# Retention and output projection of the first layer, put into the fixed order of a step pipeline

## The chip, the cores and the metric

The kernel runs on one NeuronCore of a Trainium2 chip. TensorE (PE) multiplies matrices into PSUM, VectorE (DVE) and ScalarE (ACT) work on elements, GpSimd (POOL) issues the stores here, SyncE (SP) issues the loads. The metric is the time of one execution in device microseconds. Before the change it is 2261.67 us, the median of three runs (2260.89 to 2261.71).

## The reference

A trunk of two layers over 512 tokens of width 2048, in float32. The first layer is multi-scale retention with 8 heads, the second is latent attention with 16 heads. What the change touches is the middle and the end of the first layer:

```python
def retention_branch(h, pos, w_in, gn_g, w_out):
    proj = h @ w_in                                  # 2048 -> 2048 q, 2048 k, 4096 v, 4096 g
    q, k, v, g = jnp.split(proj, ...)
    q = rope(q.reshape(B, S, RET_HEADS, RET_DK), pos)             # 8 heads of 256
    k = rope(k.reshape(B, S, RET_HEADS, RET_DK), pos) * (RET_DK ** -0.5)
    y = chunkwise_retention(q, k, v)                 # per head: (q k^T * decay) v, values of 512
    y = (y - mu) * lax.rsqrt(var + EPS)              # per head and token
    y = y.reshape(B, S, RET_WIDTH) * gn_g
    return (jax.nn.silu(g) * y) @ w_out              # 4096 -> 2048

    x = x + gate * y                                 # then the second layer's norm
```

The gate, and the shift and scale of each layer's norm, are products of a conditioning vector with `ada_w`, of which each layer has 2048 x 6144.

## The kernel before, in words

**Number format.** Each float32 operand is split into a high part and a low part (`split`, L132: ACT casts the high part, DVE subtracts for the low part). A product is three matmuls: high by high, high by low, low by high (`mm3`, L157).

**Units and steps.** Weights come in units of 512 KB: a load into a raw tile (three buffers), a split into `whi` and `wlo` (three buffers each), and 24 matmuls of 128x512. The projection into q, k, v and g of heads 0 to 7 (q and k of heads 0 to 5 only) is written as a list of `Step` objects (L619), each with a load, a prepare (the split), a multiply and a follow (the emptying of finished sums). A loop (L873) walks the list. In round i it traces, one after the other, the load of unit i + 3, the prepare of unit i + 1, the multiply of unit i, one row of a later modulation, and the follow of unit i.

**What sets an order.** The program is traced first, and a planner then puts the instructions of each engine into an order, by readiness in its own estimate of time and by the order of tracing. `behind(...)` (L414) takes this freedom away: all instructions traced in its block on the named engines are queued behind the last instruction that was traced on the same engine before the block. Instructions within one block stay free against each other. Each engine then works through its queue strictly in order; a wait holds everything behind it.

**The stretch of the change.** After the loop come three parts with no such order, left to the planner:

- q and k of heads 6 and 7 (`queries_and_keys`, L1023), 16 units.
- `retention(h)` (L923), a generator that is advanced at fixed units of the projection beside it (tables at L1035 and L1210). Its parts: load q and k, rotary product (`rope_halves`), gates' load; scores in 4 PSUM banks, times decay, split; values v loaded and split; y in 4 banks, statistics, group norm (`yn`), times gate; 16 transposes into 4 banks, scaled into `y2` (two buffers) and stored to `y2_d` in HBM.
- `out_projection` (L1047), called for n = 0 to 3. Call n multiplies two heads' `y2` (4 input units, loaded back from `y2_d` and split) with 1024 rows of the output weight, in four rounds r of 512 columns (4 units each) with 4 token banks each. Its partial sums go to `x1` in SBUF (ACT copy, L1063) and are put back into a bank when the next n needs them (ACT copy, L1103). Call n = 3 is final: rounds 0 and 1, then rounds 2 and 3 together in 8 wide units; it multiplies with the gate, adds the residual, squares for the norm and stores. Where a bank was last written by something else, a filling matmul (L1102) writes it whole before the copy; there are 8. While call n runs, heads 2n + 2 and 2n + 3 go through retention.

Banks: 4 in `acc` for the projections, 4 in `aux` for retention. The first matmul of a round needs the refilled bank; the refill needs the bank emptied. `x1_token` and `h2_pair` (L1148) finish a block of tokens: normalise, transpose, apply the second layer's scale and shift.

Of the kernel before, what the change touches and what calls it, by code (L numbers as in the profile page):

```python
# [16 lines left out]
P = 128  # L17
# [32 lines left out]
def hybrid_trunk_kernel(  # L50
# [568 lines left out]
    class Step:  # L619


        def __init__(self, load, prepare, multiply, follow=None, rows=0, sums=None, banks_free=False):
            self.load, self.prepare, self.multiply, self.follow = load, prepare, multiply, follow
            self.rows, self.sums, self.banks_free = rows, sums, banks_free

# [237 lines left out]
    later = later_modulation(lpp, [(i, s_, n) for i, s_ in ((0, 2), (1, 0)) for n in range(2)])  # L863
    fetched = []
    for i in range(3):
        with behind(S_):
            steps[i].load()
    queued(steps[0].prepare)
# [4 lines left out]
    for i, step in enumerate(steps):  # L873
        clock[0] = i
        if i + 3 < len(steps):
            with behind(S_):
                steps[i + 3].load()
        if i + 1 < len(steps):
            with behind(V_, A_):
                steps[i + 1].prepare()  # L880
# [16 lines left out]
        with behind(V_, A_):  # L897
            step.follow()
    assert next(later, None) is None and not fetched
    sum_modulation(0)  # L900
    use_modulation()
    lp.__exit__(None, None, None)


    l1 = tc.tile_pool(name="l1", bufs=1)
    l1p = l1.__enter__()

    cos, sin = rot(l1p, "cos"), rot(l1p, "sin")
    for n, t in enumerate((cos, sin)):
        nc.sync.dma_start(t, tables_d[n * P : (n + 1) * P, :])  # L910

    def rope_halves(b1, b2, dst1, dst2, name):
        t1, t2, t3, t4 = (tmp(f"{name}_t{i}") for i in range(4))
        DVE.tensor_mul(t1, b1, cos)
        DVE.tensor_mul(t4, b1, sin)
        DVE.tensor_mul(t2, b2, sin)
        DVE.tensor_mul(t3, b2, cos)
        DVE.tensor_sub(t1, t1, t2)
        split(t1, dst1[:, 0, :], dst1[:, 1, :])
        DVE.tensor_add(t3, t3, t4)  # L920
        split(t3, dst2[:, 0, :], dst2[:, 1, :])

    def retention(h, own, own2=None):  # L923

        def fetch(src_d, r0, tag, bufs, name):
            t = l1p.tile([P, T], F32, tag=tag, bufs=bufs, name=name)
            nc.sync.dma_start(t, src_d[r0 : r0 + P, :])
            return t

        dec = l1p.tile([P, T], F32, tag="dec", bufs=1, name=f"dec_{h}")  # L930
        nc.sync.dma_start(dec, decay[h])
        qk = []
        for n in range(2):
            raws = [fetch(qk_d, (4 * h + 2 * n + j) * P, "ld", 4, f"qk_{h}_{n}_{j}") for j in range(2)]
            dst = [(own2 or own)(f"qk_{h}_{n}_{j}p") for j in range(2)]
            rope_halves(*raws, *dst, f"rope_{h}_{n}")
            qk.append(dst)
        q, k = qk
        sg = [fetch(g_d, h * T + j * P, "sg", 5, f"sg_{h}_{j}") for j in range(4)]
        yield  # L940
        s_hl = []
        for m in range(NT):
            n = T - m * P
            ps = aux(f"s_{h}_{m}")
            for j in range(2):
                mm3(
                    ps[:, :n],
                    act_block(k[j], m),
                    (q[j][:, 0, m * P :], q[j][:, 1, m * P :]),
                    j == 0, j == 1,  # L950
                )
            st = tmp(f"s_{h}_{m}f")
            DVE.tensor_mul(st[:, :n], ps[:, :n], dec[:, :n])
            if m < 3:
                dst = k4b(f"sT_{h}_{m}")
                s_hl.append((dst[:, 0, :n], dst[:, 1, :n]))
                if m == 1:
                    spare = dst
            else:
                s_hl.append((spare[:, 0, 384:512], spare[:, 1, 384:512]))  # L960
            split(st[:, :n], *s_hl[m])
        v = []
        for t in range(NT):
            raw = fetch(v_d, h * T + t * P, "ld", 4, f"v_{h}_{t}r")
            v.append(own(f"v_{h}_{t}"))
            split(raw, v[t][:, 0, :], v[t][:, 1, :])
        yield
        ys, stats = [], small(f"bn_{h}", 2 * NT)
        for i in range(NT):
            ps = aux(f"y_{h}_{i}")  # L970
            for m in range(i + 1):
                o = (i - m) * P
                mm3(ps, (s_hl[m][0][:, o : o + P], s_hl[m][1][:, o : o + P]), act_row(v[m]), m == 0, m == i)
            st = l1p.tile([P, 6], F32, tag="st6", bufs=4, name=f"st_{h}_{i}")
            DVE.bn_stats(out=st, in_=ps)
            DVE.bn_aggr(out=stats[:, 2 * i : 2 * i + 2], in_=st)
            ys.append(ps)
        var = small(f"var_{h}", NT)
        DVE.tensor_copy(var, stats.rearrange("p (i s) -> p i s", s=2)[:, :, 1])
        r = rsqrt(var, NT, 1.0, f"gn_{h}")  # L980
        nmr = small(f"nmr_{h}", NT)
        DVE.scalar_tensor_tensor(
            out=nmr, in0=stats.rearrange("p (i s) -> p i s", s=2)[:, :, 0], scalar=-1.0, in1=r,
            op0=ALU.mult, op1=ALU.mult,
        )
        yn = []
        for i in range(NT):
            y = l1p.tile([P, T], F32, tag="yn", bufs=4, name=f"yn_{h}_{i}")
            ACT.activation(y, ys[i], AF.Identity, bias=nmr[:, i : i + 1], scale=r[:, i : i + 1])
            if h > 0:  # L990
                DVE.tensor_mul(y, y, sg[i])
            yn.append(y)
        yield
        for j in range(4):
            ps = aux(f"yT_{h}_{j}")
            for i in range(NT):
                PE.transpose(ps[:, i * P : (i + 1) * P], yn[i][:, j * P : (j + 1) * P], ident)
            y2 = l1p.tile([P, T], F32, tag="y2", bufs=2, name=f"y2_{h}_{j}")
            gn = gn_c[:, h * 4 + j : h * 4 + j + 1]
            if h > 0:  # L1000
                ACT.activation(y2, ps, AF.Identity, scale=gn)
            else:
                DVE.scalar_tensor_tensor(out=y2, in0=ps, scalar=gn, in1=sg[j], op0=ALU.mult, op1=ALU.mult)
            r0 = (h * 4 + j) * P
            POOL.dma_start(y2_d[r0 : r0 + P, :], y2)
        yield

    def hooks(table, otherwise=None):
        def each(i):
            if otherwise is not None and i not in table:  # L1010
                otherwise()
            for gen in table.get(i, ()):
                next(gen, None)

        return each

    n_odd = [0]

    def odd(name):
        n_odd[0] += 1  # L1020
        return l1p.tile([P, 2, T], F32R, tag="odd1" if n_odd[0] > 2 else "odd0", bufs=2, name=name)

    def queries_and_keys(h, each, evac):  # L1023
        run(
            chunk(
                [(lambda u=u: load_w(qk_parts(h, u), 2, 512, f"qk{h}_{u}"), [2 * u, 2 * u + 1]) for u in range(8)],
                [acc(f"qk{h}_{b}") for b in range(4)],
                lambda w, ki, kt, b: w_block(w, ki, b), lambda w, ki, kt, b: act_row(hT[kt]), evac,
            ),
            each=each,  # L1030
        )

    r_ = (retention(0, k4), retention(1, k4, odd))
    for h, table in (
        (6, {0: r_[:1], 3: r_, 5: r_[:1], 7: r_}),  # L1035
        (7, {1: r_[1:], 3: r_[1:]}),
    ):

        def qk_keep(b, ps, h=h):
            st = tmp(f"qk{h}_st{b}") if h == 6 else l1p.tile([P, T], F32, tag="yn", bufs=4, name=f"qk{h}_st{b}")  # L1040
            ACT.copy(st, ps)
            POOL.dma_start(qk_d[(4 * h + b) * P : (4 * h + b + 1) * P, :], st)

        queries_and_keys(h, hooks(table), qk_keep)
# [131 lines left out]
    def x1_token(t):  # L1176
# [5 lines left out]
        if t == 2:  # L1182
            h2_pair(0, 0, 8)
# [349 lines left out]
```

## Time and profile before

| | |
|---|---|
| median of three runs | 2261.67 us |
| profiled execution | 2259.02 us, span 2257.2 us |
| TensorE busy | 2190.1 us, 97% of the span |
| VectorE, ScalarE busy | 1514.2 us (67%), 1006.8 us (45%) |
| granted clock of TensorE | 0.995 of full speed |
| the stretch of the change | 948.3 us (first product of q and k of head 6) to 1510 us (last product of the output projection) |

A row of a group of instructions reads: line, engine, operation, tile written from tiles read, shapes, how many; then busy time in us and mean ns of one; then how long the engine was idle just before them, and which engine, tile and line ended that. A row of the order in time begins with the start and the duration, both in us from the start of the span, and has the idle time before it in square brackets. [...]

### The profile page before, as it was taken

What the parts mean: (1) busy time and instruction counts of PE and PEld (TensorE: products, weight loads), DVE (VectorE), ACT (ScalarE), POOL (GpSimd) and SP (SyncE); (2) the same over time, 40 slices, a digit from 0 to 9 for tenths busy, and PEclk for the clock granted to TensorE, in tenths of its full rate; (3) what the DMA queues carried; (4) which work ended last, traced back from release to release, by engine and by line L of the source; (5) the groups of instructions that cost most, each with busy time, mean ns of one, the idle gap of its engine ahead of it and who ended that gap; (6) DMA issues with size and microseconds to landing.
All of it is one profiled execution on the core that took longest, in us unless ns stands there. A gap on an engine that the chain in (4) does not pass through costs nothing.

```text
span 2257.2 us, 28012 instructions
## 1 busy us (share of the span) xinstructions
PE 2190.1 (97%) x10202; PEld 1817.5 (81%) x10202; DVE 1514.2 (67%) x2242; ACT 1006.8 (45%) x1510; POOL 132.7 (6%) x237
## 2 busy tenths in 40 slices
PE   5999999999999999999999999999999999999997
PEld 4887888888888888878878888778888888888886
DVE  7988867676676789675677673455454377777545
ACT  5664433434343444444445454554322255555433
POOL 1000000100000000001000000010000000000000
PEclk9999999999999999999999999999999999999999
DMA  9974685767767678766767664542466432235433
GB/s 342 348 238 161 197 292 188 267 209 252 237 221 251 222 246 277 259 222 197 250 214 244 209 204 141 180 147 89 134 221 224 155 102 80 85 99 175 153 120 117
DMA packets 243564, 449.73 MB, mean 199 GB/s; under 512 B 22024, under 2 KB 95840, under 8 KB 243424
## 3 DMA queue, kind: packets, MB, share of 16 engines
q1 hardware_dynamic: 228016, 400.88, 54.6%
q0 software_dynamic: 14976, 46.78, 5.3%
q8 instruction: 80, 1.31, 0.2%
q14 instruction: 60, 0.49, 0.1%
q10 hardware_dynamic: 432, 0.27, 0.0%
HBM read 396.98 MB, written 50.87 MB: 198 GB/s over the span
## 4 chain that ended last, share of the span: by engine, by line
PE 64%; issue 14%; DVE 8%; DMA 8%; ACT 5%; POOL 1%; SPq 0%; ACTq 0%; POOLq 0%; DVEq 0%
PE o L159 4%; PE o L160 4%; PE o L161 4%; PE qk L161 3%; PE qk L160 3%; PE qk L159 3%; PE g L159 3%; PE g L161 3%; PE g L160 3%; DMA aw<-in_ada_w_dram 2%; PE x L692 2%; PE y L693 2%; PE x L693 2%; PE y L691 2%; PE y L692 2%
## 5 line engine op out<-in xcount | busy, mean ns | idle before, releaser
L159 PE MATMUL o<-o_w_hi,o_h 128*128 128x512 f32 x768 | 301.8, 393 | 8.4 <-ACT o L1103 7.2
L160 PE MATMUL o<-o_w_lo,o_h 128*128 128x512 f32 x768 | 299.2, 390 | 0.0
L161 PE MATMUL o<-o_w_hi,o_l 128*128 128x512 f32 x768 | 299.0, 390 | 0.0
L134 DVE TENSOR_TENSOR o_w_lo<-o_w_raw,o_w_hi 128x1024 fp32r<-128x1024 f32 x96 | 117.3, 1223 | 129.3 <-ACT o_w_hi L133 129.2
L159 PEld LDWEIGHTS o<-o_w_hi,o_h 128*128 128x128 f32 x768 | 144.2, 188 | 42.1 <-ACT o L1103 9.8
L161 PEld LDWEIGHTS o<-o_w_hi,o_l 128*128 128x128 f32 x768 | 144.2, 188 | 30.7 <-DVE o_l L134 0.6
L160 PEld LDWEIGHTS o<-o_w_lo,o_h 128*128 128x128 f32 x768 | 144.3, 188 | 28.7
L826 DVE SCALAR_TENSOR_TENSOR mod_am<-mod_aw,cact,mod_am 128x1024 f32<-128x1024 f32 x120 | 153.6, 1280 | 12.4 <-DMA mod_aw<-in_ada_w_dram 11.8
L133 ACT CAST o_w_hi<-o_w_raw 128x1024 fp32r<-128x1024 f32 x96 | 101.1, 1054 | 110.2 <-PE o L161 91.2
L161 PE MATMUL qk<-hT,qk_l 128*128 128x512 f32 x320 | 125.0, 391 | 0.4 <-DVE qk_l L134 0.4
L159 PE MATMUL qk<-hT,qk_h 128*128 128x512 f32 x320 | 125.4, 392 | 0.0
L160 PE MATMUL qk<-hT,qk_h 128*128 128x512 f32 x320 | 124.5, 389 | 0.0
L134 DVE TENSOR_TENSOR o_l<-o_in,o_h 128x1024 fp32r<-128x1024 f32 x40 | 49.0, 1225 | 86.0 <-ACT o_h L133 85.9
L159 PE MATMUL g<-h,g_hi 128*128 128x512 f32 x256 | 100.6, 393 | 1.1 <-ACT ckv_n L1230 1.1
L160 PE MATMUL g<-h,g_hi 128*128 128x512 f32 x256 | 99.6, 389 | 0.0
L161 PE MATMUL g<-h,g_lo 128*128 128x512 f32 x256 | 99.6, 389 | 0.0
L134 DVE TENSOR_TENSOR g_lo<-g_raw,g_hi 128x1024 fp32r<-128x1024 f32 x32 | 39.2, 1225 | 81.0 <-ACT g_hi L133 81.0
L370 DVE SCALAR_TENSOR_TENSOR am<-aw,cact,am 128x512 f32<-128x512 f32 x118 | 88.7, 752 | 3.6
L133 ACT CAST g_hi<-g_raw 128x1024 fp32r<-128x1024 f32 x32 | 33.7, 1053 | 114.2 <-PE g L160 106.2
L133 ACT CAST o_h<-o_in 128x1024 fp32r<-128x1024 f32 x40 | 42.0, 1052 | 90.1 <-PE o L160 61.2
L133 ACT CAST qk_h<-qk_r 128x1024 fp32r<-128x1024 f32 x40 | 41.4, 1050 | 83.8 <-PE qk L160 70.5
L134 DVE TENSOR_TENSOR qk_l<-qk_r,qk_h 128x1024 fp32r<-128x1024 f32 x40 | 48.7, 1222 | 37.4 <-ACT qk_h L133 37.4
(1355 smaller groups left out, 5678.6 us busy)
## 6 DMA issues: line engine op xcount, KB each, us to landing
mod_aw<-in_ada_w_dram SPq DMA_DIRECT2D x128, 512.0 KB, 5.1
aw<-in_ada_w_dram SPq DMA_DIRECT2D x128, 256.0 KB, 6.0
o_w_raw<-in_ret_w_out_dram SPq DMA_DIRECT2D x64, 512.0 KB, 4.4
qk_r<-in_ret_w_in_dram SPq DMA_DIRECT2D x80, 256.0 KB, 4.0
g_raw<-in_mla_w_in_dram SPq DMA_DIRECT2D x32, 512.0 KB, 3.7
o_w_raw<-in_mla_w_out_dram SPq DMA_DIRECT2D x32, 512.0 KB, 3.7
qk_raw<-in_ret_w_in_dram SPq DMA_DIRECT2D x48, 256.0 KB, 3.9
qk_d<-qk_st POOLq DMA_DIRECT2D x32, 256.0 KB, 4.1
```

The lines of the kernel that those rows point to most:

```text
L133: ACT.copy(hi, src)
L134: DVE.tensor_sub(lo, src, hi.bitcast(F32))
L159: PE.matmul(o, lhs[0], rhs[0], start=first and not seeded, stop=False, skip_group_check=seeded)
L160: PE.matmul(o, lhs[0], rhs[1], start=False, stop=False, skip_group_check=seeded)
L161: return PE.matmul(o, lhs[1], rhs[0], start=False, stop=last, skip_group_check=seeded)
L370: DVE.scalar_tensor_tensor(out=am, in0=aw[:, k % 2], scalar=ck, in1=am, op0=ALU.mult, op1=ALU.add)
L691: PE.matmul(banks[b], a[0], w[0], start=first, stop=False, skip_group_check=True)
L692: PE.matmul(banks[b], a[0], w[1], start=False, stop=False, skip_group_check=True)
L693: PE.matmul(banks[b], a[1], w[0], start=False, stop=True, skip_group_check=True)
L826: DVE.scalar_tensor_tensor(out=am, in0=aw, scalar=ck, in1=am, op0=ALU.mult, op1=ALU.add)
```

## The change

The three parts become steps of the same loop.

- q and k of heads 6 and 7 are 16 more steps. The output projection is 4 blocks of 16 steps, one unit each (`round_steps`; in the last block, 4 steps for the wide units and 4 that finish one block of tokens each, `one_token`).
- A step may carry work beside its own, in three lists: `load` (SP), `form` (DVE and ACT) and `multiply` (TensorE).
- `retention(h)` returns ten pieces. `place` puts them into ten steps of a block that follow one another: the first head of a block from step 0, the second from step 6.
- The rows of the remaining modulation are fetched for fixed steps (`light`).
- The output projection's input units go to a tile of their own with one buffer (`in`), before three raw buffers that they shared with the weights. They are loaded two steps ahead of their use.
- Emptying and refill of a bank are in the follow of a round's last step. In the last block, 4 of the 8 filling matmuls are left out, residuals and gates are loaded at fixed steps, and the first half of the first transposes stands ahead of the last 12 products.

```diff
+        return [
+            {"load": lambda: load_qk(0)},
+            {"load": lambda: load_qk(1), "form": lambda: rope(0, 0)},
+            {"form": lambda: rope(0, 1)},
+            {"load": lambda: load_v(0), "form": lambda: rope(1, 0)},
+            {"load": load_gates, "form": lambda: rope(1, 1), "multiply": scores},
+            {"load": lambda: load_v(2), "form": decay_scores},
+            {"form": split_v, "multiply": values},
+            {"form": group_norm},
+            {"form": gate, "multiply": transposes},
+            {"form": store},
+        ]
...
+    def kept_then(n, r, after):
+        def done(t):
+            keep_sums(n, r, t)
+            if after[0] > 0:
+                seed(*after, t)
+
+        return done
+
+    for n in range(3):
+        block = []
+        for r in range(4):
+            block += round_steps(n, r, kept_then(n, r, (n, r + 1) if r < 3 else (n + 1, 0)))
+        for i in range(2):
+            place(retention(2 * n + 2 + i, big), block, 6 * i)
+        light(block, (0, 1, 2, 3, 4, 6, 9, 10, 12, 14, 15))
+        steps += block
...
+    def o1_input(n, u):
+
+        raw = []
+        r0 = (4 * n + u) * 2 * P
+
+        def load():
+            raw.append(l1_tile("in", 1, f"o1_in{n}_{u}", (P, 2, T)))
+            nc.sync.dma_start(raw[0], y2_d[r0 : r0 + 2 * P, :].rearrange("(k p) n -> p k n", p=P))
+
+        def prepare():
+            o1_in[n, u] = big(f"o1_h{n}_{u}"), big(f"o1_l{n}_{u}")
+            split(raw[0], *o1_in[n, u])
+
+        return load, prepare
...
+            load, prepare = o1_input(n, u)
+            i = n_o1 + 16 * n + u
+            steps[i - 2].beside["load"].append(load)
+            steps[i].units[0] = (steps[i].units[0][0], lambda a=steps[i].units[0][1], b=prepare: (a(), b()))
...
+    def one_token(t, r):
+        if (t, r) == (3, 3):
+            queued(h2_pair, 0, 0, 8)
+        for u in range(4, 8):
+            o1_product(3, wide[u][0], u, 0, t, r, slice((r - 2) * T, (r - 1) * T), u == 7)
...
     for i, step in enumerate(steps):
         clock[0] = i
...
+        with behind(S_):
+            while n_loaded < min(n_prepared + 3, len(loads)):
+                loads[n_loaded]()
+                n_loaded += 1
+            for load in step.beside["load"]:
+                load()
+        n_prepared += prepare_for(i + 1)
+        with behind(V_, A_):
+            use_modulation()
+            for form_ in step.beside["form"]:
+                form_()
+        with behind(T_):
+            if step.banks_free:
+                sum_modulation()
+        with behind(T_):
+            step.multiply()
+        with behind(T_):
+            for multiply in step.beside["multiply"]:
+                multiply()
         with behind(V_, A_):
             for add in fetched:
                 add()
...
+        with behind(V_, A_, T_):
             step.follow()
```

More of the change, by code (lines that the diff above doesn't have):

```diff
@@ L861, in use_modulation, with l1_tile, odd @@
             POOL.dma_start(gate_d[i : i + 1, part : part + 512], row[0:1, :])
-    later = later_modulation(lpp, [(i, s_, n) for i, s_ in ((0, 2), (1, 0)) for n in range(2)])
-    fetched = []
[L865 to L868, printed above, removed]
+    pools = {}
+    def l1_tile(tag, bufs, name, shape=(P, T), dt=F32):
+        return pools["l1"].tile(list(shape), dt, tag=tag, bufs=bufs, name=name)
+    def odd(name):
+        n_odd[0] += 1
+        return l1_tile("odd1" if n_odd[0] > 2 else "odd0", 2, name, (P, 2, T), F32R)
@@ new lines, in place, with light @@
+    def place(pieces, block, first):
+        for i, piece in enumerate(pieces):
+            for kind, fn in piece.items():
+                block[first + i].beside[kind].append(fn)
+    def light(block, which):
+        for i in which:
+            block[i].rows = 1
+        for i in range(4):
+            block[i].banks_free = True
+    block = []
+    for h in (6, 7):
+        block += plain_steps(
+            8, 2, qk_parts_of(h), 512, f"qk{h}", acc, 4,
+            lambda w, ki, kt, b: w_block(w, ki, b), lambda w, ki, kt, b: act_row(hT[kt]),
+            lambda b, ps, h=h: keep_rows(
+                ps, qk_d, (4 * h + b) * P, f"qk{h}_st{b}",
+                own=tmp if h == 6 else lambda name: l1_tile("yn", 4, name),
+            ),
+        )
@@ new lines, in hybrid_trunk_kernel, with x1_block, seed @@
+    n_p = len(steps)
+    light(block, ())
+    place(retention(0, k4), block, 0)
+    place(retention(1, k4, odd), block, 6)
+    steps += block
+    x1 = []
+    ss1 = [small(f"x1_ss{t}", 4) for t in range(NT)]
+    NU1 = 4
+    def x1_block(t, r):
+        if not x1:
+            x1.extend([k4(f"x1_{t_}_{j}", F32) for j in range(2)] for t_ in range(NT))
+        return x1[t][r // 2][:, r % 2, :]
+    o1_banks = {}
+    def seed(n, r, t):
+        o1_banks[n, r, t] = (aux if n == 3 and r % 2 else acc)(f"o1_{n}_{r}_{t}")
+        if n > 0:
+            ACT.copy(o1_banks[n, r, t], x1_block(t, r))
@@ new lines, in o1_product, with round_steps, multiply, follow @@
+    def o1_product(n, w, kt, ki, t, r, cols=slice(0, T), last=False):
+        hi, lo = o1_in[n, kt // 2]
+        a = tuple(p[:, kt % 2, t * P : (t + 1) * P] for p in (hi, lo))
+        o = o1_banks[n, r, t]
+        first = n == 0 and kt == 0
+        for i, j in ((0, 0), (0, 1), (1, 0)):
+            PE.matmul(
+                o, a[i], w[j][:, ki, cols], start=first and i + j == 0, stop=last and i == 1, skip_group_check=True
+            )
+    def round_steps(n, r, done):
+        res = []
+        for u in range(NU1):
+            w, unit = o1_unit(n, r, u, 2, T)
+            step = Step()
+            step.units = [unit]
+            def multiply(u=u, w=w):
+                order = [(ki, t) for ki in range(2) for t in range(NT)]
+                if u in (0, NU1 - 1):
+                    order = [(ki, t) for t in range(NT) for ki in range(2)]
+                for ki, t in order:
+                    if (n, r, t) not in o1_banks:
+                        seed(n, r, t)
+                    o1_product(n, w, 2 * u + ki, ki, t, r, last=u == NU1 - 1 and ki == 1)
+            def follow(u=u):
+                if u == NU1 - 1:
+                    for t in range(NT):
+                        done(t)
+            step.multiply, step.follow = multiply, follow
+            res.append(step)
+        return res
@@ new lines, in kept_then @@
+    def kept_then(n, r, after):
[5 more added lines that the diff above has]
+    for n in range(3):
+        block = []
+        for r in range(4):
[3 more added lines that the diff above has]
+        light(block, (0, 1, 2, 3, 4, 6, 9, 10, 12, 14, 15))
+        steps += block
@@ L912, in rope_halves @@
[L912 to L1044, printed above, removed]
+    assert next(later, None) is None and not fetched and not ripe and not summed
```

306 lines of the change are left out of this document (231 added, 75 removed).

## The prediction

> **What bounds the kernel now.** I read the page's head and its engine line first, then the busy time in two stretches (the input projection of layer 1, which already runs as a step pipeline, and the stretch that the change rewrites), then what TensorE's instructions waited for there, then the order in time of single engines, and the chain that ended last.
>
> ```profile
> span 2257.2 us, 28012 instructions
> PE 2190.1 (97%) x10202; PEld 1817.5 (81%) x10202; DVE 1514.2 (67%) x2242; ACT 1006.8 (45%) x1510; POOL 132.7 (6%) x237
> ```
> ```profile
> 250.00:850.00 600.00, 600.00 (x2641) 495.49 (x2640) 432.52 (x487) 245.34 (x291) 34.35 (x64) 1.00 0.71 236
> 948.30:1510.00 561.70, 548.29 (x2539) 454.55 (x2539) 346.92 (x521) 256.84 (x395) 41.15 (x66) 1.00 0.62 206
> ```
> (Columns: the stretch, its length, then busy time of PE, weight loads, DVE, ACT and POOL, the granted clock, the share of DMA.) TensorE is the bound. The old step pipeline never lets it idle; the rewritten stretch is idle for 561.7 - 548.3 = 13.4 us. The groups that waited (last column: idle before them):
> ```profile
> L159 PE MATMUL o<-o_w_hi,o_h 128*128 128x512 f32 x512 | 201.7, 394 | 8.4 <-ACT o L1103 7.2 <-ACT x L1063 1.0 <-ACT qk_st L1041 0.2
> L1156 PE MATMUL x1T<-ident,x 128*128 128x128 f32 x64 | 11.1, 297 | 4.7 <-DVE h2f L1173 3.3 <-DVE o_g L1071 1.4
> ```
> Most of it is the refill of a sum's bank by ScalarE (L1103). TensorE's busy time overstates its work, because matmuls overlap. The order in time gives the real pace:
> ```profile
> 944.85 3.63 PE L839 MATMUL mod_ps<-ones,mod_am 128*128 128x1 f32 x32
> ...
> 949.59 0.63 PE L160 MATMUL qk<-hT,qk_hi 128*128 128x512 f32 x1
> ...
> 954.17 0.39 PE L159 MATMUL qk<-hT,qk_hi 128*128 128x512 f32 x1
> ...
> 966.18 0.39 PE L161 MATMUL qk<-hT,qk_lo 128*128 128x512 f32 x1
> 966.41 0.39 PE L159 MATMUL s<-qk_0p,qk_0p 128*128 128x512 f32 x1
> ...
> 967.83 0.50 PE L161 MATMUL s<-qk_0p,qk_0p 128*128 128x512 f32 x1 [0.80 <-DVE qk_0p L134]
> ...
> 971.25 0.45 PE L159 MATMUL qk<-hT,qk_hi 128*128 128x512 f32 x1
> ...
> 1001.38 1.91 PE L997 MATMUL yT<-ident,yn 128*128 128x128 f32 x16
> ```
> 54 products start in 954.17 to 966.18: one each 0.2266 us. So a unit of weights (24 products) is 5.44 us of TensorE, the values of a head (30) 6.8, its scores 971.25 - 966.41 - 0.8 - some 0.1 = 3.9, its transposes 1.91 less some 0.2 of overlap, 1.7. Everything below is measured against these 5.44 us, not against 24 x 0.39 = 9.4.
>
> **What it removes.** Work of the stretch, counted from the code: 384 qk, 1536 o, 240 y and 8 filling products (L1102), 2168 x 0.2266 = 491.3; scores 8 x 3.9 = 31.2; transposes 8 x 1.7 = 13.3; some 32 small sums like those at 944.85, 3.6; the first x1 transposes, about 2. Together 541.4, of 561.7: 20.3 us are lost, the 13.4 of idle and 6.9 that busy time hides. About 4 of these I leave standing, an estimate, for the changes from one kind of product to another, which stay. So at most 16.3 us go, and 4 of the 8 filling products, 4 x 0.23 = 0.9: **-17.2 us**.
>
> **What it costs nothing.** Splits, rotary products, gates and loads keep their number and sizes; they run on queues with idle time (DVE 347 and ACT 257 of 562). That cover is gone wherever one queue must finish a list inside one step, which is the next part. The modulation rows move to fixed steps (33 places for 32 rows); their sums stay 128x1 products. The first x1 transposes move in front of the last 12 products of o; they are paid either way, between -4.7 (the idle shown goes) and +3.3 (its h2f part comes again); I take 0. POOL keeps its queue; it only issues.
>
> **What it adds.** In each step DVE and ACT now take, in order: split of the next unit, the retention pieces, the modulation row, and only then the emptying of the sums (follow). What is late in a piece holds the sums, and these hold TensorE. Paces of these engines, by starts in a row:
> ```profile
> 1188.05 0.68 DVE L134 TENSOR_TENSOR v<-v_2r,v 128x512 fp32r<-128x512 f32 x1
> 1188.65 0.68 DVE L134 TENSOR_TENSOR v<-v_3r,v 128x512 fp32r<-128x512 f32 x1
> 1189.33 1.23 DVE L134 TENSOR_TENSOR o_l<-o_in,o_h 128x1024 fp32r<-128x1024 f32 x1
> 1190.47 1.28 DVE L826 SCALAR_TENSOR_TENSOR mod_am<-mod_aw,cact,mod_am 128x1024 f32<-128x1024 f32 x1
> 1191.67 1.22 DVE L134 TENSOR_TENSOR o_w_lo<-o_w_raw,o_w_hi 128x1024 fp32r<-128x1024 f32 x1
> ```
> ```profile
> 1182.17 1.11 ACT L1103 COPY o<-x 128x512 f32<-128x512 f32 x2
> 1183.21 0.59 ACT L1063 COPY x<-o 128x512 f32<-128x512 f32 x1
> ```
> DVE: 0.60 for a 512-wide operation, 1.14 for the low part of a unit, 1.20 for a row. ACT: 0.5 for a copy. The store, an input load's cycle, and the group norm:
> ```profile
> 1349.21 1.26 ACT L1001 ACTIVATE y<-yT,vcol 128x512 f32<-128x512 f32 x2
> ...
> 1355.55 0.69 ACT L1001 ACTIVATE y<-yT,vcol 128x512 f32<-128x512 f32 x1 [3.00 <-DMA y_d<-y]
> ...
> 1356.85 0.69 ACT L1001 ACTIVATE y<-yT,vcol 128x512 f32<-128x512 f32 x1
> ```
> ```profile
> 1047.17 3.70 DMA o_in<-y_d
> 1050.89 1.07 ACT o_h L133
> 1051.98 1.24 DVE o_l L134
> ```
> ```profile
> DMA to landing us min/median/max: 2.3/4.0/7.2
> ```
> ```profile
> 1152.68 0.17 DVE L976 BATCH_NORM_AGGREGATE bn<-st 128x2 f32<-128x6 f32 x1
> ```
> ```profile
> 1154.62 2.78 ACT L989 ACTIVATE yn<-y,nmr,gn_r 128x512 f32<-128x512 f32 x4 [2.12 <-DVE nmr L982]
> ```
>
> (a) Store in step 15. It begins when the first quarter of the transposes is done, 1.2 us before TensorE starts step 15, and lasts 1357.5 - 1349.2 = 8.3, because y2 has two buffers and the third waits for the first to land. The keep of bank 0 is behind it: first sum kept and refilled at -1.2 + 8.3 + 1.0 = 8.1, where TensorE wants it at 5.44. Wait **2.7** ahead of rounds n = 1, 2, 3, and **2.2** ahead of n = 0 (no refill): 10.3. Ends, with the landings of 2.3 and 7.2 in place of some 4.4: 0.6 and 5.5 each.
>
> (b) Steps 0 to 4 of a block. The last refill ends 2.9 us after TensorE starts step 0 (8 copies of 0.5 from 7.1); a cast, 1.07; only then DVE begins. Up to the emptying of step 3 it owes 7 low parts (8.0), 3 rows (3.6), two rotary halves of 4 operations and 3 of a third (11 x 0.6 = 6.6): 18.2. The input tile has one buffer, so in(u+1) is issued when in(u) is split: some 3.9 to land (3.70 in the row, 4.0 the median) and a cast of 1.07, of which 2.8 are uncovered over the two loads. 4.0 + 18.2 + 2.8 = 25.0, cast, keep and refill 1.7: 26.7, against 4 x 5.44 = 21.8: **4.9**. Behind that, 7 more copies, cast, low part and rotary half hold the scores of step 4 by **1.5**. So 6.4 in n = 1 and 2; for n = 0 without refills 2.8 + 0.5; for n = 3 (inputs, no pieces) 2.0. Sum 18.1. Ends: 0.4, if the inputs were ready and the refills early (1.2 + 1.07 + 18.2 + 1.7 = 22.2 against 21.8); twice as much, if each load takes 7.2. SP waits with the in load; behind it are rows and weights for three steps ahead, which have two steps to spare: 0.
>
> (c) Steps 7 and 8. The last bank's statistics take 0.9, the group norm's yn begin 1.9 us after them and last 2.8: to 5.6 us into step 7 ACT is at work; 8 copies to 9.6, cast to 10.7, low part to 11.8, four gates to 14.2. TensorE would be at the transposes after 2 x 5.44 = 10.9 and reaches gate 3 by 11.2: **3.0** in n = 1 and 2; 1.0 in n = 0 and 0.7 in the qk block, which have fewer copies. Sum 7.7; ends 0, if keep and refill slip in ahead of the norm, and 12, if the planner lets each of the four run as late as the dearest (3.0).
>
> Steps 5, 6 and 9 to 14: DVE owes about 5 us or less in each against 5.44 and more: 0.
>
> **Sum.** 10.3 + 18.1 + 7.7 = 36.1 added, 17.2 removed: +18.9. The profiled execution took 2259.02 (2257.2 of span and 1.8 around it); the median of the runs shown is 2261.67, 0.12% above. I forecast 2261.67 + 18.9, rounded: **2280 us**.
>
> A row on the clock: the wait in
> ```profile
> 1182.81 0.50 PE L159 MATMUL o<-o_w_hi,o_h 128*128 128x512 f32 x1 [2.43 <-ACT o L1103]
> 1183.15 0.40 PE L160 MATMUL o<-o_w_lo,o_h 128*128 128x512 f32 x1
> ```
> is followed by the full pace (0.34 us to the next start, products of 0.39 to 0.40 again), so short waits cost only themselves. [...]
>
> **The rivals.** *Faster.* The lockstep holds as it does at 250 to 850, where DVE was busy for 432.5 of 600 and TensorE never idle; here DVE has 62%. Then only -17.2 counts: 2245. Against it: at 250 to 850 no step has a store, an input cycle or a refill. It decides where (a) to (c) sum to less than 12.7 (17.2 less 4.5, the 0.2% that a measurement of this kernel can tell from no change). Chance 0.25, from 2244 to 2257.
> *No change.* (a) at its low end (2.4 in all), (b) and (c) at half (9 and 4): 15.4 of waits against 17.2: 2260. Chance 0.08.
> *Much slower.* Loads land at their long end, in a stretch whose DMA is 62% busy: 2 x 18.1 + 4 x 5.5 + 12 - 17 = +53 at most; from 2298, middle 2306. [...] Chance 0.15.
> The forecast itself: 0.52, own range 2266 to 2298.
>
> **How the numbers follow.** Faster 0.25, same 0.08, slower 0.52 + 0.15 = 0.67. Below 2247 lie about 0.12, above 2306 about 0.07.
>
> **What would show it.** In the changed kernel: waits of TensorE for ACT's refill ahead of steps 0 and 4 of each block, near 2.7 and 4.9 us; ACT's y behind DMA y_d just before the first; transposes behind the gate's DVE product, near 1.7; the fall of the 7.2 us of L1103 would show the gain. Wrong it would be if keep and refill do not follow the store and the rotary cast in ACT's order, or if the in loads land before they are asked for.

## The result and the profile after

The changed kernel takes 2300.61 us (median of six runs, 2297.33 to 2304.37); the kernel before, timed beside it, 2259.61 us (2256.82 to 2261.71). The ratio is 1.0182, 95% interval 1.0169 to 1.0195: slower by 41.0 us, where 18.9 were forecast. The profiled execution took 2304.37 us.

The head of the page and its engine line, after:

```profile
span 2302.6 us, 27929 instructions
PE 2209.8 (96%) x10198; PEld 1831.1 (80%) x10198; DVE 1521.1 (66%) x2242; ACT 1003.4 (44%) x1510; POOL 131.6 (6%) x237
```

TensorE has four matmuls fewer (the filling products) and is nevertheless busy for 19.7 us longer. The stretch of the change, from the first product of q and k of head 6 to the last of the output projection (columns as in the prediction: the stretch, its length, busy time of PE, weight loads, DVE, ACT, POOL, granted clock, DMA):

```profile
948.17:1551.20 603.03, 565.34 (x2530) 466.00 (x2531) 351.22 (x514) 250.01 (x388) 39.66 (x65) 0.96 0.57 192
```

Before it was 561.7 us long with 548.3 busy. So 41.3 us are lost here, in two parts of different kinds. TensorE idles for 603.0 - 565.3 = 37.7 us, 24.3 more than before. And nearly the same products (four filling products and five transposes fewer) keep it busy for 565.3 instead of 548.3 us, 17.0 more, at a granted clock of 0.96 where it was 1.00. The rest of the span is 4.1 us longer (2302.6 - 603.0 = 1699.6, against 2257.2 - 561.7 = 1695.5).

What TensorE waited for, from 930 to 1600 us (what waited, for what, us in all, times, longest):

```profile
PE o L1112 <- ACT o L1053: 15.2, 6, 5.5
PE s L159 <- ACT qk_1p L133: 15.0, 4, 4.4
PE o L1112 <- ACT x L1056: 3.4, 1, 3.4
PE x1T L1222 <- DVE h2f L1239: 3.2, 1, 3.2
PE o L1112 <- ACT qk_st L578: 2.4, 1, 2.4
PE o L1112 <- DVE o_l L134: 0.9, 2, 0.6
```

The refills (L1053, line 1103 before) took the place that the forecast gave them, ahead of steps 0 and 4. As dear is a wait that the forecast did not have at all: the second head's scores, in step 10, for the high part of the last rotary half.

The order in time of TensorE, after; first step 4 of block 1, then the scores of step 10:

```profile
1226.44 0.79 PE L1112 MATMUL o<-o_whi,o_h 128*128 128x512 f32 x1 [5.12 <-ACT o L1053]
1227.02 0.63 PE L1112 MATMUL o<-o_wlo,o_h 128*128 128x512 f32 x1
1227.45 0.63 PE L1112 MATMUL o<-o_whi,o_l 128*128 128x512 f32 x1
...
1229.96 0.40 PE L1112 MATMUL o<-o_whi,o_l 128*128 128x512 f32 x1
...
1287.22 0.80 PE L159 MATMUL s<-qk_1p,qk_1p 128*128 128x512 f32 x1 [4.44 <-ACT qk_1p L133]
```

Here is the second kind of loss. After the wait of 5.12 us the products start 0.43 us apart instead of 0.227, until 1229.96: 8 distances in 3.52 us that should have taken 1.81, so 1.7 us are paid after the wait; the granted clock is 0.52 there, and 0.50 from 1094.6 to 1100.0, behind the wait of 3.42 us. Counted in this way over 7 us behind each, the seven waits of 2.99 us and more (step 4 three times, step 10 three times, one boundary) carry 16.3 of the 17.0 us.

Why step 10 waits is seen on ScalarE and VectorE of the same kernel:

```profile
1280.70 0.69 ACT L990 ACTIVATE y<-yT,vcol 128x512 f32<-128x512 f32 x1 [4.29 <-DMA y_d<-y]
...
1282.29 1.03 ACT L133 CAST o_whi<-o_r 128x1024 fp32r<-128x1024 f32 x1
1286.55 0.62 ACT L133 CAST qk_1p<-rope_t 128x512 fp32r<-128x512 f32 x1 [3.22 <-DVE rope_t L884]
```
```profile
1283.36 1.23 DVE L134 TENSOR_TENSOR o_wlo<-o_r,o_whi 128x1024 fp32r<-128x1024 f32 x1 [5.02 <-ACT o_whi L133]
1284.50 0.69 DVE L882 TENSOR_TENSOR rope_t<-qk_r,sin 128x512 f32<-128x512 f32 x1
```

The first head of a block stores in step 9 of the block. The store's third quarter needs one of two `y2` tiles and waits 4.29 us for its DMA; the cast of the next unit (L133) is queued behind it on ScalarE; VectorE stands idle for 5.02 us until that cast is done, and only then makes its low part and the rotary half that step 10's scores need. The forecast saw this store for the second head, in step 15, and not for the first.

### The profile page after: what moved, and what is told of

Same layout as the page of the kernel before. It is cut to its first block, busy times and chain, and to the rows that moved or that the text cites. A ratio compares the mean times of both kernels' runs of the same rounds, so it can differ in the third digit from the quotient of the medians.

```text
span 2302.6 us, 27929 instructions
## 1 busy us (share of the span) xinstructions
PE 2209.8 (96%) x10198; PEld 1831.1 (80%) x10198; DVE 1521.1 (66%) x2242; ACT 1003.4 (44%) x1510; POOL 131.6 (6%) x237
## 4 chain that ended last, share of the span: by engine, by line
PE 62%; issue 26%; DVE 5%; ACT 3%; DMA 3%; POOL 1%; SPq 0%; POOLq 0%; ACTq 0%; DVEq 0%
PE o L1112 4%; PE qk L161 3%; PE qk L159 3%; PE qk L160 3%; PE g L159 3%; PE g L160 3%; PE g L161 3%; PE o L161 2%; PE o L159 2%; PE o L160 2%; PE x L695 2%; PE x L696 2%; PE y L696 2%; PE x L694 2%; PE y L695 2%
## 5 line engine op out<-in xcount | busy, mean ns | idle before, releaser
L1112 PE MATMUL o<-o_whi,o_h 128*128 128x512 f32 x496 | 199.3, 403 | 21.0 <-ACT o L1053 15.2
L1112 PE MATMUL o<-o_whi,o_l 128*128 128x512 f32 x496 | 195.9, 396 | 0.9 <-DVE o_l L134 0.9
L1112 PE MATMUL o<-o_wlo,o_h 128*128 128x512 f32 x496 | 196.6, 397 | 0.1
L159 PE MATMUL qk<-hT,qk_h 128*128 128x512 f32 x448 | 176.5, 394 | 0.0
L160 PE MATMUL qk<-hT,qk_h 128*128 128x512 f32 x448 | 175.3, 391 | 0.0
L1112 PEld LDWEIGHTS o<-o_whi,o_h 128*128 128x128 f32 x496 | 95.6, 193 | 44.2 <-ACT o L1053 18.2
L1112 PEld LDWEIGHTS o<-o_wlo,o_h 128*128 128x128 f32 x496 | 95.7, 193 | 20.1 <-DVE o_wlo L134 0.9
L159 PE MATMUL o<-o_w_hi,o_h 128*128 128x512 f32 x256 | 100.1, 391 | 0.0
L160 PE MATMUL o<-o_w_lo,o_h 128*128 128x512 f32 x256 | 99.9, 390 | 0.0
L161 PE MATMUL o<-o_w_hi,o_l 128*128 128x512 f32 x256 | 99.5, 390 | 0.0
L159 PEld LDWEIGHTS qk<-hT,qk_h 128*128 128x128 f32 x448 | 84.8, 189 | 17.8 <-issue 0.2
L160 PEld LDWEIGHTS qk<-hT,qk_h 128*128 128x128 f32 x448 | 84.7, 189 | 18.0 <-issue 0.5
```

The lines of the kernel that those rows point to most:

```text
L159: PE.matmul(o, lhs[0], rhs[0], start=first and not seeded, stop=False, skip_group_check=seeded)
L160: PE.matmul(o, lhs[0], rhs[1], start=False, stop=False, skip_group_check=seeded)
L161: return PE.matmul(o, lhs[1], rhs[0], start=False, stop=last, skip_group_check=seeded)
L1112: PE.matmul(o, a[i], w[j][:, ki, cols], start=first and i + j == 0, stop=last and i == 1, skip_group_check=True)
```

## The experiments

All are edits of the changed kernel but the last control, which edits the kernel before. The windows rows are of the same stretch, from the first product of q and k to the last of the output projection.

### Four buffers for the store

```diff
-                y2 = l1_tile("y2", 2, f"y2_{h}_{j}")
+                y2 = l1_tile("yn", 4, f"y2_{h}_{j}")
...
-                     own=tmp if h == 6 else lambda name: l1_tile("yn", 4, name),
+                     own=tmp,
```

> Scaled y2 tiles take the four buffers of yn in place of two of their own (q and k of head 7 are kept in tmp instead of yn), so the third store no longer waits for the first to land. Queue theory (ACT in order: store, then keep, refill, casts): the waits of TensorE ahead of the first steps of a block (2.4, 3.0, 0.4) and at the scores of a block's second head (2.2, 3.9, 4.4, 4.4) go, with half clock behind three of them, 1.7 each: 20.7 + 5.1, about -26 us, 2275. Rival (VectorE has too much to do per step; the store is only where it shows): the store is not VectorE's, so the waits stay or move, 2297 to 2303.

2272.14 us (2271.68 to 2272.72), ratio 1.0052 [1.0037, 1.0067]: 28.5 us of the 41.0 are gone. Its stretch, and all waits above 1.3 us that are left in it:

```profile
946.75:1521.39 574.64, 556.86 (x2531) 458.70 (x2530) 351.83 (x514) 250.24 (x389) 40.21 (x66) 0.98 0.60 202
```
```profile
1089.11 0.80 PE L1112 MATMUL o<-o_whi,o_h 128*128 128x512 f32 x1 [3.41 <-ACT x L1056]
...
1211.54 0.80 PE L1112 MATMUL o<-o_whi,o_h 128*128 128x512 f32 x1 [4.63 <-ACT o L1053]
...
1334.86 0.80 PE L1112 MATMUL o<-o_whi,o_h 128*128 128x512 f32 x1 [4.41 <-ACT o L1053]
```

Idle time falls from 37.7 to 574.6 - 556.9 = 17.8 us, and busy time, with the same products, from 565.3 to 556.9. The waits of step 10 and of the boundaries of the blocks are both gone, so both hung on the store's two tiles. The rival, that the step lists alone hold the scores, falls.

### The modulation rows elsewhere; the rotary half behind the refill

Two ways to relieve step 3, at whose end the banks are emptied and refilled for step 4. The first takes VectorE's three rows out of steps 1 to 3:

```diff
-        light(block, (0, 1, 2, 3, 4, 6, 9, 10, 12, 14, 15))
+        light(block, (0, 4, 5, 6, 8, 9, 10, 12, 13, 14, 15))
```

> The modulation rows of steps 1, 2 and 3 of each block stand at steps 5, 8 and 13 instead. VectorE has 1.2 us less in each of the steps where it is late. Queue theory: two rows stand ahead of the rotary half that holds the keep of step 3, one of them partly in the gap of an input load: 2.0 less wait ahead of step 4 in each of three blocks, -6, and half clock behind one to three of them, -2 to -5: 2290 to 2293. Rival (the input loads alone set the time of these steps): 2298 to 2302.

2291.32 us (2288.96 to 2296.9), ratio 1.0145 [1.0128, 1.0162]: 9.3 us less, within what was expected. The waits of step 4 are 2.56, 3.58 and 3.79 us instead of 3.42, 5.12 and 5.49, which is 4.1 in all.

The second traces step 3's rotary half behind the emptying and refill instead of ahead of them:

```diff
-            for form_ in step.beside["form"]:
+            for form_ in step.beside["form"] if not step.late else ():
                 form_()
...
         with behind(V_, A_, T_):
             step.follow()
+        if step.late:
+            with behind(V_, A_):
+                for form_ in step.beside["form"]:
+                    form_()
...
+        block[3].late = True
```

> In step 3 of the three blocks the keep and refill are traced ahead of the rotary half instead of behind it; no work changes. Queue theory: ACT empties the banks when TensorE is done with them, the waits ahead of step 4 (3.4, 5.1, 5.5) go with half clock behind each, 14.0 + 5.1 = -19 us, 2281, and the scores of step 4 are just in time. Rival (VectorE and the input loads are late whatever the order): the wait moves to the scores of step 4, 0 to -5 us, 2295 to 2300.

2286.04 us (2284.1 to 2287.11), ratio 1.0112 [1.0097, 1.0128]: 14.6 less, where the theory had 19 and the rival 5 at most. The waits for the refill fall to 0, 0.28 and 0.82 us, and a smaller one comes in their place for the scores of step 4, which the theory had taken to be just in time; here in block 0 and block 1:

```profile
1098.19 0.50 PE L159 MATMUL s<-qk_1p,qk_1p 128*128 128x512 f32 x1 [1.20 <-ACT qk_1p L133]
...
1223.92 0.50 PE L159 MATMUL s<-qk_1p,qk_1p 128*128 128x512 f32 x1 [1.35 <-ACT qk_1p L133]
```

Waits of 14.0 us went and 3.9 came (1.20, 1.35 and 1.34); with the 1.1 left that is 9.0 less, and the time fell by more, since the products behind these three waits follow at the full pace. The two runs show that what stands ahead of the emptying in VectorE's and ScalarE's lists sets the wait of step 4, and the second that holding the scores there costs less than holding the sums.

### Is the slow pace the price of idling?

Matmuls that nobody needs were put into the waits. First into those ahead of step 4 and of step 10's scores at once, in the changed kernel:

```diff
+        block[3].beside["multiply"].append(lambda n=n: fill(n, 3, 12))
+        block[10].beside["multiply"].insert(0, lambda n=n: fill(n, 10, 12))
```

> 12 matmuls into a spare bank behind step 3 and 12 ahead of the second head's scores in step 10, in the three blocks of the output projection that have retention beside them: TensorE has 2.7 us of work inside each of its six longest waits, which stay as long in all. [...]

2297.59 us (2294.12 to 2303.2), ratio 1.0167 [1.015, 1.0183]: 3.0 less, where six times the 1.7 us counted behind the wait of 5.12 us would be 10; and the two kernels' runs overlap. In its stretch, 72 such products among the rest:

```profile
948.19:1543.30 595.11, 572.33 (x2601) 471.26 (x2602) 351.23 (x515) 249.70 (x388) 39.67 (x65) 0.98 0.58 194
```

Without them (72 x 0.227 = 16.3) TensorE is busy for 556.0 us, 9.3 less than in the changed kernel; idle time and fillers together are 22.8 + 16.3 = 39.1, 1.4 more than the changed kernel's idle time. So the pace recovers in part. Slow products stayed behind a wait of 3.02 us at the end of block 0, which had no fillers, and behind two waits that the fillers left: 2.62 us ahead of block 1's step 10 and 2.75 us ahead of block 2's step 4. This run leaned towards idling as the cause and did not settle it.

The cleaner form stands on the kernel with four store buffers, where only three long waits are left:

```diff
+        block[3].beside["multiply"].append(lambda n=n: fill(n, 3, 12))
```

> On top of the four store buffers (2272.1 us), twelve matmuls that nobody needs stand behind step 3 of each block, in the waits for step 4's refill (3.41, 4.63 and 4.41 us there, each followed by 11 or 12 products at about half the pace). Nothing of VectorE's or ScalarE's work changes. Theory (the slow products are the price of an idle stretch, some 34 products x 0.2 us = 6.8 us in all): the waits shrink by 12 x 0.227 = 2.7 us each, to 0.7, 1.9 and 1.7, no slow products follow them, and the time falls to 2264 to 2268. Rival (the slow pace comes from something else at this place, as operands that arrive late): the slow products stay and the time stays at 2271 to 2273.

2268.32 us (2265.89 to 2273.84), ratio 1.0041 [1.0027, 1.0055]: 3.8 less than without the fillers by the medians, just outside the 2264 to 2268 expected; one of its five runs is slower than all of those without fillers. The profiled run is its fastest, and its stretch shows the mechanism:

```profile
946.41:1514.66 568.25, 559.42 (x2566) 460.58 (x2566) 351.37 (x515) 249.69 (x389) 40.20 (x66) 0.99 0.61 204
```
```profile
1325.88 2.88 PE L1154 MATMUL fill<-o_h 128*128 128x512 f32 x12
...
1330.89 0.50 PE L1112 MATMUL o<-o_whi,o_h 128*128 128x512 f32 x1 [2.13 <-ACT o L1053]
...
1331.45 0.40 PE L1112 MATMUL o<-o_whi,o_l 128*128 128x512 f32 x1
```

Nothing was made faster; useless work was added; and in the profiled runs the stretch is 6.4 us shorter (568.25 against 574.64). Behind the wait of block 2's step 4, now 2.13 us, the first product takes 0.50 instead of 0.80 and the full pace follows at once. Operands that arrive late can't explain that. So the slow pace at this place is the price of the idle stretch ahead of it.

### A second buffer for the input units

```diff
-            raw.append(l1_tile("in", 1, f"o1_in{n}_{u}", (P, 2, T)))
+            raw.append(l1_tile("in", 2, f"o1_in{n}_{u}", (P, 2, T)))
```

This stands on the four store buffers too.

> On top of the four store buffers (2272.1 us), the output projection's input units have two buffers instead of one, so that a load no longer waits for the split of the unit before it. Theory (the forecast's part (b): 2.8 us of the input loads are uncovered by step 4): the waits ahead of step 4 (3.41, 4.63, 4.41 us) fall by up to 2.8 us each, the slow products behind them go, the small waits for an input's split (3.5 us in all) go, and the time falls to 2253 to 2259. Rival (VectorE's list alone, low parts, modulation rows and rotary halves, sets step 4): these waits stay within 0.7 us, only the small ones go, and the time is 2267 to 2270.

2261.06 us (2259.11 to 2264.23), ratio 1.0010 [1.0001, 1.0019]: 11.1 less than 2272.14, between the two theories. The waits of step 4:

```profile
1083.40 0.50 PE L1112 MATMUL o<-o_whi,o_h 128*128 128x512 f32 x1 [0.85 <-ACT x L1056]
...
1201.31 0.80 PE L1112 MATMUL o<-o_whi,o_h 128*128 128x512 f32 x1 [4.40 <-ACT o L1053]
...
1322.89 0.79 PE L1112 MATMUL o<-o_whi,o_h 128*128 128x512 f32 x1 [3.12 <-ACT o L1053]
```

3.41 became 0.85, 4.63 became 4.40, 4.41 became 3.12. These waits alone mislead, because the small waits for inputs ahead of them went too (1.22 and 0.30 us in block 1), so TensorE comes to step 4 earlier. From the first product of a block to the first of its step 4 it takes 22.8 us instead of 28.4 in block 0, 26.8 instead of 28.7 in block 1 and 25.1 instead of 26.4 in block 2. So the loads held step 4 in all three blocks, by 5.7, 1.9 and 1.3 us. That is 3.0 in the mean, near the forecast's 2.8, but unevenly spread; in block 1 and block 2, which start with refills, most of the wait is still there, and the moved rows and the late rotary half above show that it is the lists'.

### Together

The first and the third edit at once; of their diffs the two lines that matter:

```diff
+                y2 = l1_tile("yn", 4, f"y2_{h}_{j}")
...
+        block[3].late = True
```

> The two changes that gained most, together: four store buffers, and in step 3 of a block the rotary half behind the emptying and refill of the banks instead of ahead of them. If their gains add up (28.5 and 14.6 us, the second less the small part that the first already holds), the time is 2256 to 2260: step 4's refill waits go from 3.4, 4.6 and 4.4 us to under 1, waits of some 1.3 us for the scores of step 4 come in their place, and the slow products behind go. Rival (the queue's delay is only handed on to the scores of step 4 in full): 2265 to 2272.

2257.48 us (2256.45 to 2259.95), ratio 0.9993 [0.9984, 1.0002]: as expected, and level with the kernel before. With the second input buffer and the moved rows as well:

```diff
+            raw.append(l1_tile("in", 2, f"o1_in{n}_{u}", (P, 2, T)))
...
+        light(block, (0, 4, 5, 6, 8, 9, 10, 12, 13, 14, 15))
```

> All four: four store buffers, two input buffers, the modulation rows of steps 1, 2 and 3 moved to steps 5, 8 and 13, and step 3's rotary half behind the refill. If the fixed order is good once no queue has more than a step's work inside a step, TensorE idles less than 6 us in the stretch and the time is 2249 to 2256, below the kernel before (2260). Rival (the rotary products, gates and rows only hold another step): new waits in steps 5, 8 or 10, and 2258 to 2266.

2250.74 us (2248.59 to 2253.42), ratio 0.9959 [0.9946, 0.9971]: 49.9 us below the changed kernel, and faster than the kernel before. Its stretch, and the longest wait left in it:

```profile
948.32:1500.24 551.92, 547.91 (x2530) 453.65 (x2530) 349.67 (x514) 249.82 (x388) 39.67 (x65) 1.00 0.63 209
```
```profile
1205.90 0.50 PE L159 MATMUL s<-qk_1p,qk_1p 128*128 128x512 f32 x1 [1.04 <-ACT qk_1p L133]
```

Idle time is 4.0 us, and the busy time, 547.9, is that of the kernel before (548.3). So this is what the fixed order with its queues put right is worth in the stretch: 13.4 - 4.0 = 9.4 us of idle, and next to nothing of busy time.

### The first transposes earlier

On top of that version, 12 products earlier:

```diff
-        if (t, r) == (3, 3):
+        if (t, r) == (3, 2):
             queued(h2_pair, 0, 0, 8)
```

> On top of the version with all four edits (2250.74 us), the first half of the first transposes of x1 stands 12 products earlier. What follows the output projection takes 750.4 us there, against 747.2 in the kernel before, whose transposes begin one token earlier. Theory (the transposes' VectorE and ScalarE work then lies beside products, and the wait of 3.34 us for it and the slow products behind shrink): 2246 to 2250. Rival (that wait is for the second token pair's normalising, which does not move): 2250 to 2253, with a new wait of up to 1.4 us ahead of the earlier transposes.

2250.35 us (2249.13 to 2253.99), ratio 0.9965 [0.9953, 0.9977]: no change, the rival. The wait behind the output projection is there as before the edit:

```profile
1515.10 0.66 PE L1224 MATMUL x1T<-ident,x 128*128 128x128 f32 x4 [3.32 <-DVE h2f L1241]
```

So it is not the start of the first half that sets it. What does was not tried.

### The store's buffers in the kernel before

```diff
-            y2 = l1p.tile([P, T], F32, tag="y2", bufs=2, name=f"y2_{h}_{j}")
+            y2 = l1p.tile([P, T], F32, tag="yn", bufs=4, name=f"y2_{h}_{j}")
...
-            st = tmp(f"qk{h}_st{b}") if h == 6 else l1p.tile([P, T], F32, tag="yn", bufs=4, name=f"qk{h}_st{b}")
+            st = tmp(f"qk{h}_st{b}")
```

> A control: the kernel before, with the store tiles on the group norm's four buffers as in the other runs, nothing else. In its old order the store's third quarter waits for the first to land as well (3.00 and 4.06 us of ScalarE at 1355.55 and 1169.90), but TensorE's refill waits come to 7.2 us in all. Theory (the order written out by the planner lets the emptying slip in between, so the store holds little): 2254 to 2260, and the fixed order with its queues put right (2250.7) stays ahead. Rival (the store is as dear in the old order, and the gain of the four-part version is only the buffers'): 2249 to 2253.

2274.24 us (2273.2 to 2275.0), ratio 1.0065 [1.0052, 1.0077]: slower by 15 us, which neither theory had. One head's scores now wait on TensorE, and VectorE's rotary product for the same head waits before them:

```profile
1071.54 0.79 PE L159 MATMUL s<-qk_0p,qk_0p 128*128 128x512 f32 x1 [10.47 <-ACT qk_0p L133]
```
```profile
1063.46 0.69 DVE L916 TENSOR_TENSOR rope_t<-qk,sin 128x512 f32<-128x512 f32 x1 [4.51 <-DMA qk_d<-qk_st]
```

`rope_t` and `qk_st` are both `tmp` tiles, of which there are six, and this edit moves head 7's `qk_st` there. So the shared tiles have a part in it: the rotary product waits 4.51 us for a store of `qk_st` to land. In the kernel before the same scores stand later, at 1082.83, behind products that need no rotary half; the planner's new order has a part in it too, and how much is each one's stays open. So the edit that gives 28.5 us in the fixed order costs 15 in the planned one. This edit alone does not bring the kernel before to 2250.74; four store buffers that share no tile with anything else were not tried there.

## Why the prediction was right and wrong

Its direction held, and so did the likeliest case's mechanism: lists that don't fit into a step hold the emptying and refill, and TensorE waits there. The size was under half of what came. Step by step:

**The clock: the step that failed.** "so short waits cost only themselves". The row was of a wait of 2.43 us, and the waits forecast at 4.9 were priced by it, at nothing beyond themselves. Measured, 17.0 us of busy time were added, and the filler run on the four buffers shows that idling is what causes it there. There were more long waits than the two of 4.9 us, seven, and each cost 16.3 / 7 = 2.3 us in the mean beyond itself. The trace of the kernel before had a row against the reading, behind the stretch:

```profile
1523.44 0.66 PE L1156 MATMUL x1T<-ident,x 128*128 128x128 f32 x4 [2.29 <-DVE h2f L1173]
...
1527.28 0.63 PE L161 MATMUL cq<-cq_hi,h 128*128 128x512 f32 x1
1527.70 0.63 PE L159 MATMUL cq<-cq_hi,h 128*128 128x512 f32 x1
```

Behind waits of 2.29, 0.59 and 0.36 us close together the products already start 0.42 us apart there.

**"Steps 5, 6 and 9 to 14: 0": the other step that failed.** It counted VectorE's own work, about 5 us a step, which was right (32.2 us busy in steps 9 to 14 of block 1, 5.4 each), and left out that ScalarE's store in step 9 holds the cast that VectorE's next operation waits for. Measured 15.0: 2.2, 3.9, 4.4 and 4.4. The mechanism was the forecast's own part (a), at the other place where a store stands.

**(a), store in step 15: 10.3 forecast, 5.8 measured.** ScalarE's order, after, at the end of block 0 and of block 1:

```profile
1187.94 1.26 ACT L990 ACTIVATE y<-yT,vcol 128x512 f32<-128x512 f32 x2 [3.02 <-PE yT L982]
1192.25 0.69 ACT L990 ACTIVATE y<-yT,vcol 128x512 f32<-128x512 f32 x1 [3.04 <-DMA y_d<-y]
1195.46 0.69 ACT L990 ACTIVATE y<-yT,vcol 128x512 f32<-128x512 f32 x1 [2.53 <-DMA y_d<-y]
1196.05 1.06 ACT L1056 COPY x<-o 128x512 f32<-128x512 f32 x2
...
1320.59 1.27 ACT L990 ACTIVATE y<-yT,vcol 128x512 f32<-128x512 f32 x2 [2.96 <-PE yT L982]
1324.33 0.69 ACT L990 ACTIVATE y<-yT,vcol 128x512 f32<-128x512 f32 x1 [2.48 <-DMA y_d<-y]
...
1325.89 1.06 ACT L1056 COPY x<-o 128x512 f32<-128x512 f32 x2
```

The first time the store holds the copies for 1196.05 - 1187.94 = 8.1 us (8.3 forecast) and TensorE waits 2.99; the second time the DMA lands sooner, it is 1325.89 - 1320.59 = 5.3 us, and nothing waits. The four waits of TensorE were 2.39, 2.99, 0 and 0.38. Right in its mechanism, and one row of the kernel before was taken for all four.

**(b), steps 0 to 4: 18.1 forecast, 14.9 measured.** Refills of step 4: 3.42, 5.12 and 5.49, against 2.8, 4.9 and 4.9. The inputs' own waits, 0.64 and 0.24 us, came in blocks 0 and 2, and the 2.0 forecast for the last block did not come. The scores of step 4 did not wait (3.5 forecast), since TensorE came to them late by the refill's wait: when the late rotary half took that wait away, they waited 3.9 in all. The input run shows that the 2.8 us for the loads inside that sum are right in the mean and were 5.7, 1.9 and 1.3.

**(c), steps 7 and 8: 7.7 forecast, 1.5 measured.** After, on ScalarE, VectorE and TensorE in block 1:

```profile
1257.97 2.78 ACT L969 ACTIVATE yn<-y,nmr,gn_r 128x512 f32<-128x512 f32 x4 [0.73 <-DVE nmr L963]
...
1266.54 2.49 DVE L975 TENSOR_TENSOR yn<-yn,sg 128x512 f32<-128x512 f32 x4
...
1261.30 0.50 PE L1112 MATMUL o<-o_whi,o_h 128*128 128x512 f32 x1 [0.60 <-ACT o L1053]
...
1267.28 2.46 PE L982 MATMUL yT<-ident,yn 128*128 128x128 f32 x16
```

The gates' chain was right: 13.9 us from TensorE's start of step 7 (1255.1) to the last gate's end, where 14.2 were worked out. TensorE came to the transposes after 12.2 instead of 10.9, in part because it had waited 0.60 for the refill, so little was left to wait for.

**The removal: 17.2 forecast.** The best version shows 9.4 of idle gone, at most 13.4 could go, and its busy time is that of before. The "6.9 that busy time hides" do not go; that is the part of the term that was too large. (Its sum has a slip besides: 8 x 1.7 is 13.6, not 13.3.)

**The first transposes: 0 forecast, within -4.7 and +3.3.** What follows the stretch grew by 4.2 us in the changed kernel, 751.4 against 747.2. The h2f wait came again as the upper end had it, 3.2 us in one piece where the kernel before had 3.3 in three, so it is not what grew: TensorE's busy time there grew by 2.2 us and its idle time by 2.0. Five transposes fewer lie inside the stretch (12 recorded against 17). That the term was past its upper end is measured; why was not settled.

The waits came out near their sum by offsetting errors: 36.1 forecast, 37.7 of idle time measured, of which 15.0 in a place forecast at nothing. Then 37.7 - 13.4 + 17.0 = 41.3, where the forecast had 36.1 - 17.2. Of the rivals, "faster" fell with every queue that held a step, and its size came within reach only when four things were put right; "much slower" had its size nearly right and its cause wrong: stores at the four boundaries held the copies for 8.5, 8.1, 5.3 and 5.5 us, no longer than the 8.3 assumed but for 0.2.

## What to carry to other kernels

When planned work becomes a fixed order, list for every step what each in-order queue issues, with the waits of its DMAs in it, and look at every place where the same piece stands: a store that waits for its own buffer delays all that is behind it on that engine and, through the next cast, the other engine too (here 4.29 us on ScalarE and 5.02 us of idle time on VectorE). Price a long wait of TensorE together with the slow pace behind it (here the seven of 2.99 us and more cost some 2.3 us each beyond themselves), and read all rows that speak on it, not the one that fits. And before such an order is given up, buffers and the place of a piece within its step are worth trying: four small edits took 49.9 us off the same order.

## What the runs showed of the hardware

In these runs the slow pace does not begin at a fixed length of wait, nor always at the wait's end. In the run with the moved rows a wait of 2.56 us was followed by four quick products and then by slow ones:

```profile
1090.86 0.50 PE L1112 MATMUL o<-o_whi,o_h 128*128 128x512 f32 x1 [2.56 <-ACT x L1056]
1091.20 0.40 PE L1112 MATMUL o<-o_wlo,o_h 128*128 128x512 f32 x1
...
1092.17 0.63 PE L1112 MATMUL o<-o_whi,o_l 128*128 128x512 f32 x1
1092.60 0.63 PE L1112 MATMUL o<-o_whi,o_h 128*128 128x512 f32 x1
```

From 940 to 1600 us of the changed kernel and of the runs with the fillers in it, the moved rows and the late rotary half, every wait of 3.1 us and more (3.11 to 5.49) was followed by such products, at once or within 1.5 us. Between 2.15 and 3.06 us it went either way. After 2.56 and 2.99 us they came; after another wait of that same run, and after one in the control on the kernel before, they did not:

```profile
1147.83 0.50 PE L159 MATMUL s<-qk_1p,qk_1p 128*128 128x512 f32 x1 [3.04 <-ACT qk_1p L133]
```
```profile
1190.02 0.50 PE L159 MATMUL o<-o_w_hi,o_h 128*128 128x512 f32 x1 [3.06 <-ACT o L1103]
```

The shortest single wait with a slow stretch behind it is one of 2.15 us, ahead of the scores of the run with the moved rows:

```profile
1022.45 0.50 PE L159 MATMUL s<-qk_1p,qk_1p 128*128 128x512 f32 x1 [2.15 <-ACT qk_1p L133]
...
1024.87 0.53 PE L161 MATMUL s<-qk_1p,qk_1p 128*128 128x384 f32 x1
```

The same product of the changed kernel, behind a wait of 2.22 us, took 0.33 us. And in the filler run on the four buffers two waits of 1.43 and 0.30 us, 1.3 us apart, were followed by a slow stretch too. So the length of a single wait did not decide alone here.
